# Four sums of weight quarters made by adding transfers that GpSimd begins, in a two-layer hybrid decoder on one Trainium2 core

## The chip, the core and the metric

The kernel runs on one core of a Trainium2 chip. A core has five engines that run their own in-order queues and meet at semaphores: TensorE (PE, with its weight loads shown as PEld), VectorE (DVE), ScalarE (ACT), GpSimd (POOL) and SyncE (SP). Sixteen DMA engines move data between HBM and the on-chip memory SBUF, or within SBUF. TensorE writes its sums to the small memory PSUM. The metric is the device time of one execution in microseconds; lower is better.

## The reference

Two layers, each one pre-norm mixer with three head groups that share one input projection. Cut to what matters here:

```python
def _layer(x, ...):
    h = _rmsnorm(x, norm_g)
    proj = h @ w_in            # (512, 2048) @ (2048, 7696)
    ...
    mix = jnp.concatenate([y_conv, y_sb, y_gla], axis=-1)
    return x + mix @ w_out     # (512, 2048) @ (2048, 2048)

for l in range(2):
    h = _layer(h, ...)
```

The change touches only how the weights of the last product, `mix @ w_out`, are prepared.

## The kernel before

Every projection is cut into tiles of 256 output columns. A tile of weights is 2048 x 256 in float32; it is fetched by two SyncE transfers of 1 MB into a staging buffer `st` of shape 128 x 16 x 272 (`fetch`, line 332; there are two such buffers). ScalarE squares it to find its size (`wmax`, line 347), GpSimd adds over the partitions (`wscale`, line 355, the all-reduce of line 362), VectorE turns that into a scale of a power of two (lines 363 to 379), and then each value is split into a float16 high part, made by ScalarE, and a float16 low part, made by VectorE. A product of two split numbers takes three float16 matmuls. The tiles of split weights, `wh` and `wl`, come in three buffers each. `weights()` (line 467) is called at each tile: it starts the fetch of the tile two ahead and the splitting of the next one. A staging buffer is free for its next fetch when the last split that reads it is done.

The output projection of a layer has eight column groups. In groups 3, 4 and 6 of the first layer and 3, 4, 5 and 6 of the second (`QUICK`, line 30), seven in all, the product is made from 2 x 2 blocks with seven block products in place of eight (`project_quick`, line 686; its matmuls are line 698, 48 for each product, 336 for a group). For this the weights enter as the four quarters b11, b12, b21, b22, each a 128 x 8 x 128 view of the staging buffer in rows of 512 bytes, and as sums of them. `wsums` (line 436) makes these sums in place and splits them: part 0 is b11, part 3 is b22, part 1 is b11 + b12 + b22, part 2 is b12 + b22, part 4 is b21, part 5 is b11 + b12, part 6 is b11 + b12 + b22 + b21. Parts 0 and 1 share one pair of weight buffers, 2 and 3 the next, 4 and 5 the third; part 6 has its own small pair (`e` and `ga`). A split is one ScalarE instruction (line 450) and one VectorE instruction (line 451). The sums depend on each other through the quarters that they overwrite. The products are written in the source in the order of parts 0, 1, 2, 3, 4, 5, 6; ScalarE and VectorE carry the partial results out of PSUM on the way (lines 709 to 727), and line 1247 adds the residual.

Outside the kernel's first stretch a scheduler puts the instructions of each engine in order when the program is built. It places them by times that it assumes, so a change of one instruction also moves others. In the program before, GpSimd begins no transfers; SyncE and ScalarE do.

Of the kernel before, what the change touches and what calls it, by code (L numbers as in the profile page):

```python
# [11 lines left out]
ALU = mybir.AluOpType  # L12
# [27 lines left out]
def hybrid_trunk(ctx, tc, x, norm_g, w_in, conv_w, conv_b, sb_qn_g, sb_kn_g,  # L40
                 gla_w_up, gla_b_up, gla_on_g, w_out, out):
    nc = tc.nc
    V, S, G, T = nc.vector, nc.scalar, nc.gpsimd, nc.tensor
# [23 lines left out]
    def nm(s):  # L67
        uid[0] += 1
        return f"{s}_{uid[0]}"
# [4 lines left out]
    def wk(shape, tag, bufs=None, dt=F32):  # L74
        return work.tile(shape, dt, tag=tag, name=nm(tag), bufs=bufs)
# [347 lines left out]
    def load_(i):  # L423

        with tc.issue_after(lasthi[i - 1].ins):
            for h in range(2):
                wmax(i, h)
        wscale(i)
        if i in quick:
            wsums(i)  # L430
            return
        for h in range(2):
            whi(i, h)
            wlo(i, h)

    def wsums(i):

        sc = scales[i]
        b11, b12, b21, b22 = (whole[i][:, r::2, c * P:(c + 1) * P] for r in range(2) for c in range(2))
        parts = loaded[i][0]  # L440
        for _ in range(3):
            a = [wpool.tile([P, HK, GX], F16, tag=t, name=nm(t)).rearrange("p k c -> p (k c)") for t in ("wh", "wl")]
            parts.extend([p_[:, n * HK * P:(n + 1) * HK * P] for p_ in a] for n in range(2))
        parts.append([wk([P, HK * P], t, dt=F16) for t in ("e", "ga")])
        for n in range(7):
            parts[n] = [a.rearrange("p (k c) -> p k c", c=P) for a in parts[n]]

        def split(b, n):
            h_, l_ = parts[n]
            hi = S.activation(h_, b, AF.Copy, scale=sc)  # L450
            V.scalar_tensor_tensor(l_, b, sc, h_, ALU.mult, ALU.subtract)  # L451
            return hi


        split(b11, 0)
        V.tensor_tensor(b11, b11, b12, ALU.add)
        split(b22, 3)
        V.tensor_tensor(b12, b12, b22, ALU.add)
        V.tensor_tensor(b22, b11, b22, ALU.add)
        split(b22, 1)  # L460
        lasthi[i] = split(b12, 2)
        V.tensor_tensor(b22, b22, b21, ALU.add)
        split(b21, 4)
        split(b11, 5)
        split(b22, 6)
# [845 lines left out]
```

## Time and profile before

| | before |
|---|---|
| median of 3 runs | 1720.0 us (1718.39 to 1720.52) |
| the profiled execution | 1721.89 us |
| its span | 1720.1 us |
| TensorE clock granted, mean | 0.997 |
| DMA, mean over the span | 205 MB, 119 GB/s |
| HBM read, written | 173.36 MB, 8.39 MB |

All rows of the trace come from one execution. Its span is the time between the first and the last instruction; 1.8 us lie around it. A row of a group of instructions gives line, engine, operation, output and input tile with buffer numbers left out, count, then busy time and the mean duration of one in ns, and the idle time of the engine ahead of them with what ended it. A row of the waits names who waited for whom, the total in us, how often, and the longest. A row of the windows gives the stretch, its length, the busy time of PE, PEld, VectorE, ScalarE and GpSimd with the number of instructions, the granted clock, the share of time in which the DMA engines were busy, and GB/s. A row of the timeline or of the chain of waits begins with start and length in us from the start of the span. A row of a transfer ends with the median time from its issue until the data has landed.

### The profile page before, as it was taken

To read this page: it belongs to the slowest core of one execution; us is meant where nothing else is said; L and a number is where in the kernel's file an instruction comes from. 1 tells how busy PE (TensorE), PEld (TensorE's weight loads), DVE (VectorE), ACT (ScalarE), POOL (GpSimd) and SP (SyncE) were. 2 spreads that over 40 slices of the span, in tenths; PEclk is the share of its full clock that TensorE was granted. 3 is DMA by queue.
4 is the path that set the end of the run, shared out by engine and by line. 5 is a ranking of instruction groups with operands and counts; after the bars stand their busy time and mean duration, and the time that the engine had idled before them with its cause. 6 is when DMAs were issued, how large, how long until landed. Compare 5 with 4: busy or idle time off the path is not lost. (4 is left out here: it accounts for less than half of the span.)

```text
span 1720.1 us, 32415 instructions
## 1 busy us (share of the span) xinstructions
PE 1702.0 (99%) x13770; PEld 1227.2 (71%) x13770; DVE 1166.7 (68%) x2149; ACT 1022.4 (59%) x1243; POOL 63.5 (4%) x104
## 2 busy tenths in 40 slices
PE   7999999999999999999999999999999999999998
PEld 5744557878787764799986454668686868548998
DVE  8566897566666656786675588974656566567883
ACT  7558676555555555566655575864555555545661
POOL 1100000000000000000010000000000000000000
PEclk9999999999999999999999999999999999999999
DMA  7323321344444445145544231223544433343441
GB/s 251 98 98 98 99 98 54 113 120 126 119 121 123 129 123 153 61 156 181 181 116 148 83 108 55 99 98 111 126 127 126 125 108 108 116 137 123 148 155 45
DMA packets 266641, 204.95 MB, mean 119 GB/s; under 512 B 93362, under 2 KB 265724, under 8 KB 265984
## 3 DMA queue, kind: packets, MB, share of 16 engines
q1 hardware_dynamic: 257488, 193.42, 37.1%
q10 hardware_dynamic: 9008, 9.45, 1.6%
q8 instruction: 108, 1.77, 0.4%
q14 instruction: 37, 0.30, 0.1%
HBM read 173.36 MB, written 8.39 MB: 106 GB/s over the span
## 5 line engine op out<-in xcount | busy, mean ns | idle before, releaser
L421 DVE SCALAR_TENSOR_TENSOR wl<-st,ws,wh 128x2048 f16<-128x2048 f32 (+1 forms) x138 | 324.4, 2352 | 205.3 <-ACT wh L415 205.3
L415 ACT ACTIVATE wh<-st,ws 128x2048 f16<-128x2048 f32 (+1 forms) x136 | 272.0, 2003 | 247.0 <-PE psp L633 111.0
L633 PE MATMUL psp<-wh,m 128*128 128x256 f16 x1216 | 331.5, 273 | 0.0
L632 PE MATMUL psp<-wl,m 128*128 128x256 f16 x1216 | 331.4, 273 | 0.0
L631 PE MATMUL psp<-wh,m 128*128 128x256 f16 x1216 | 331.4, 273 | 0.0
L352 ACT ACTIVATE junk<-st 128x2048 uint8<-128x2048 f32 (+1 forms) x150 | 285.5, 1903 | 4.9 <-DMA st<-in_w_out_dram 3.0
L633 PE MATMUL psp<-wh,x 128*128 128x256 f16 x768 | 209.3, 273 | 0.0
L632 PE MATMUL psp<-wl,x 128*128 128x256 f16 x768 | 209.3, 273 | 0.0
L631 PE MATMUL psp<-wh,x 128*128 128x256 f16 x768 | 209.3, 273 | 0.0
L623 PE MATMUL psp<-m,wh 128*128 128x512 f16 x512 | 194.0, 379 | 0.0
L624 PE MATMUL psp<-x,wh 128*128 128x512 f16 x512 | 194.0, 379 | 0.0
L624 PE MATMUL psp<-m,wh 128*128 128x512 f16 x512 | 194.0, 379 | 0.0
L623 PE MATMUL psp<-x,wh 128*128 128x512 f16 x512 | 194.0, 379 | 0.0
L625 PE MATMUL psp<-x,wl 128*128 128x512 f16 x512 | 193.9, 379 | 0.0
L625 PE MATMUL psp<-m,wl 128*128 128x512 f16 x512 | 193.9, 379 | 0.0
L625 PEld LDWEIGHTS <-wl 128*128 128x128 f16 x1024 | 100.2, 98 | 119.7
L624 PEld LDWEIGHTS <-wh 128*128 128x128 f16 x1024 | 100.2, 98 | 118.7 <-issue 2.6
L623 PEld LDWEIGHTS <-wh 128*128 128x128 f16 x1024 | 100.2, 98 | 117.5 <-issue 1.9
L631 PEld LDWEIGHTS <-m 128*128 128x128 f16 x1216 | 119.0, 98 | 13.9
L633 PEld LDWEIGHTS <-m 128*128 128x128 f16 x1216 | 119.0, 98 | 13.9
L632 PEld LDWEIGHTS <-m 128*128 128x128 f16 x1216 | 119.0, 98 | 13.8
L363 DVE TENSOR_SCALAR wq<-wgm 128x1 f32<-128x1 f32 x75 | 15.9, 212 | 111.1 <-POOL wgm L362 111.1
(356 smaller groups left out, 2665.0 us busy)
## 6 DMA issues: line engine op xcount, KB each, us to landing
st<-in_w_in_dram SPq DMA_DIRECT2D x120, 1024.0 KB, 7.7
st<-in_w_out_dram SPq DMA_DIRECT2D x32, 1024.0 KB, 7.6
x<-in_x_dram SPq DMA_DIRECT2D x4, 1024.0 KB, 5.1
qT<-in_x_dram ACTq DMA_DIRECT2D x8, 512.0 KB, 6.4
qT<-xs ACTq DMA_DIRECT2D x8, 512.0 KB, 3.9
xs<-x SPq DMA_DIRECT2D x14, 256.0 KB, 3.8
out_dram<-kT SPq DMA_DIRECT2D x14, 256.0 KB, 2.1
th<-za SPq DMA_TRANSPOSE x64, 3.1
```

The lines of the kernel that those rows point to most:

```text
L352: S.activation(junk(HK * n).rearrange("p (k n) -> p k n", k=HK), staged[i][h][:, :, :n], AF.Square, accum_out=peak[i][:, h:h + 1])
L363: V.tensor_scalar(m, gm[:, 0:1], gm[:, 1:2], 2.0 ** -120, ALU.add, ALU.max)
L415: lasthi[i] = S.activation(wh[:, :, :n], staged[i][h][:, :, :n], AF.Copy, scale=scales[i])
L421: V.scalar_tensor_tensor(wl[:, :, :n], staged[i][h][:, :, :n], scales[i], wh[:, :, :n], ALU.mult, ALU.subtract)
L623: T.matmul(o, wh[:, kk, cs], xh[:, :, k, :], start=st_, stop=False)
L624: T.matmul(o, wh[:, kk, cs], xl[:, :, k, :], start=False, stop=False)
L625: T.matmul(o, wl[:, kk, cs], xh[:, :, k, :], start=False, stop=en)
L631: T.matmul(o, ah[:, t, k, :], wh[:, kk, :n], start=st_, stop=False, skip_group_check=True)
L632: T.matmul(o, ah[:, t, k, :], wl[:, kk, :n], start=False, stop=False, skip_group_check=True)
L633: T.matmul(o, al[:, t, k, :], wh[:, kk, :n], start=False, stop=en, skip_group_check=True)
```

## The change

In `wsums` the four VectorE additions become four transfers that GpSimd begins. Each reads one quarter and adds it into another, in the same places of the staging buffer as before; the splits and their source order stay.

```diff
         split(b11, 0)
-        V.tensor_tensor(b11, b11, b12, ALU.add)
+        G.dma_start(out=b11, in_=b12, accum_op=ALU.add)
         split(b22, 3)
-        V.tensor_tensor(b12, b12, b22, ALU.add)
-        V.tensor_tensor(b22, b11, b22, ALU.add)
+        G.dma_start(out=b12, in_=b22, accum_op=ALU.add)
+        G.dma_start(out=b22, in_=b11, accum_op=ALU.add)
         split(b22, 1)
         lasthi[i] = split(b12, 2)
-        V.tensor_tensor(b22, b22, b21, ALU.add)
+        G.dma_start(out=b22, in_=b21, accum_op=ALU.add)
         split(b21, 4)
         split(b11, 5)
         split(b22, 6)
```

With the new times that the scheduler assumes, the built program also has other orders inside the seven groups. On TensorE the matmuls are the same, but the products of part 2 come ahead of those of part 1 and those of part 4 are partly ahead of part 3. On ScalarE and VectorE the splits of parts 4 and 5 come earlier among the splits of a group, and those of parts 2 and 1 later. On GpSimd the 28 transfers stand between the all-reduces of line 362; those of one group follow each other, and in five groups the all-reduce of the next tile stands between the third and the fourth, in two behind the fourth. Outside these groups the orders are the same but for a few neighbours.

## The prediction

> **What bounds the kernel now.** I read the busy shares of the page first, then the waits of the tensor engine, then the stretches in which seven-product groups run (windows of 20 us), then the chain of waits at the end.
>
> ```profile
> span 1720.1 us, 32415 instructions
> PE 1702.0 (99%) x13770; PEld 1227.2 (71%) x13770; DVE 1166.7 (68%) x2149; ACT 1022.4 (59%) x1243; POOL 63.5 (4%) x104
> ...
> PE psp L698 <- ACT g L709: 1.3, 1, 1.3
> PE psp L698 <- DVE g L711: 0.8, 1, 0.8
> PE psp L698 <- DVE wl L451: 0.2, 1, 0.2
> ```
>
> TensorE is busy in 99% of the span. In all seven groups (matmul line 698) it waits for the other engines 1.3 + 0.8 + 0.2 = 2.3 us. So whatever VectorE is relieved of, no more than 2.3 us can come back there: 1720.0 - 2.3 = 1717.7 us.
>
> ```profile
> 1640.00:1660.00 20.00, 20.00 (x362) 20.00 (x360) 17.04 (x25) 12.93 (x15) 0.40 (x1) 1.00 0.49 159
> 1660.00:1680.00 20.00, 19.84 (x354) 19.62 (x352) 16.88 (x24) 12.47 (x14) 0.40 (x1) 1.00 0.48 160
> ...
> 1664.71 9.15 DMA st<-in_w_out_dram
> 1673.95 2.00 ACT junk L352 x2
> 1675.95 1.05 ACT wh L450
> 1677.03 1.28 DVE wl L451
> ```
>
> The columns of the first two rows are the busy time of PE, weight load, VectorE, ScalarE and GpSimd, the clock and the DMA share. VectorE is busy 17 of 20 us and TensorE all 20: both are nearly full, with TensorE ahead. The chain rows show that a second loop closes almost as tightly: a staging buffer is released, 9.15 us of fetch, the maxima on ScalarE, the splits, release again. There is little room in which a longer splitting stage could hide.
>
> **What is removed.**
>
> ```profile
> L456 DVE TENSOR_TENSOR st<-st x7: 1218/1225/1226, 764.9 to 1665.8; 128x1024 f32<-128x1024 f32 x7
> L462 DVE TENSOR_TENSOR st<-st x7: 1216/1218/1224, 773.6 to 1679.8; 128x1024 f32<-128x1024 f32 x7
> L451 DVE SCALAR_TENSOR_TENSOR wl<-st,ws,wh x42: 1273/1278/1286, 762.5 to 1681.7; 128x1024 f16<-128x1024 f32 x42
> L450 ACT ACTIVATE wh<-st,ws 128x1024 f16<-128x1024 f32 x42 | 46.4, 1141 | 23.4 <-PE psp L698 9.7 <-DVE st L458 6.0 <-PE psp L633 3.0
> ```
>
> Four additions in each of seven groups, 28 x 1.22 = 34 us of VectorE. By the 2.3 us above, this is worth next to nothing on the path.
>
> **What is added: 28 transfers that form one chain.** Number them 1 to 4 in each group (lines 456, 458, 459, 462). Transfer 2 overwrites b12, which transfer 1 reads; transfer 3 adds b11 (result of 1) into b22, which transfer 2 reads; the split of part 1 reads the result of 3; transfer 4 overwrites b22 after that split. In the built program transfer 2 waits for the semaphore of 1, transfer 3 for that of 2, transfer 4 for that of 3 and for VectorE's half of split 1. So no two of a group overlap. With D the time from start to landing of one transfer, and a split costing 1.14 us on ScalarE plus 1.28 us on VectorE, that is 2.42:
>
> split 0 (2.42), three transfers (3D), split 1 (2.42), transfer 4 (D), ScalarE's half of split 6 (1.14) = 4D + 6.0 us from split 0 to the end of split 6.
>
> Does the next group have to wait for it? ScalarE is an in-order queue. In the order the built program gives it, split 6 of group 3 of the second layer stands ahead of split 0 of group 4, and that of group 4 ahead of split 0 of group 5: there the period is 4D + 6.0. Between groups 5 and 6 of that layer and between 3 and 4 of the first, split 0 comes ahead of split 6. In the first layer GpSimd's queue has transfer 4 ahead of the all-reduce that scales the next group, so split 0 follows the issue of transfer 4: 3D + 2.42 + 2.42 + 1.06 = 3D + 5.9, the 1.06 being the path from the all-reduce to split 0 (778.85 to 779.91 below). In the second, split 0 of group 6 needs the weight tile that parts 0 and 1 of group 5 share, so it follows product 1 of group 5, 16.09 / 6 = 2.7 us (six products in the row of 1619.05) after split 1: 3D + 2.42 + 2.42 + 2.7 = 3D + 7.5.
>
> ```profile
> 778.85 0.40 POOL L362 PARTITION_ALL_REDUCE wgm<-wm  x1 [18.26 <-ACT junk L352]
> 779.91 1.15 ACT L450 ACTIVATE wh<-st,ws 128x1024 f16<-128x1024 f32 x1 [0.88 <-DVE ws L375]
> ...
> 761.31 2.19 ACT L450 ACTIVATE wh<-st,ws 128x1024 f16<-128x1024 f32 x2 [1.21 <-DVE wp L377]
> 817.22 0.19 ACT L352 ACTIVATION_READ_ACCUMULATOR junk<-st 128x1 f32 x1
> 818.62 1.15 ACT L450 ACTIVATE wh<-st,ws 128x1024 f16<-128x1024 f32 x1 [1.21 <-DVE wp L377]
> 849.89 0.42 DVE L727 TENSOR_TENSOR g<-psp,g 128x256 f32<-128x256 f32 x1
> ...
> 1605.52 1.13 ACT L450 ACTIVATE wh<-st,ws 128x1024 f16<-128x1024 f32 x1
> 1619.05 16.09 PE psp L698 x288
> 1695.58 0.42 DVE L727 TENSOR_TENSOR g<-psp,g 128x256 f32<-128x256 f32 x1 [0.80 <-PE psp L698]
> ```
>
> *Second layer, groups 3, 4, 5, 6 in a row.* Split 0 of group 3 starts at 1605.52; nothing ahead of it changes. Before, the last product of group 6 ended at 1695.58 (the VectorE instruction that reads it). After: 1605.52 + two periods of 4D + 6.0, one of 3D + 7.5, then 4D + 6.0 for group 6, VectorE's half of split 6 (1.28) and the last product, 2.7: 1605.5 + 15D + 25.5 + 4.0 = 1635.0 + 15D. Delay 15D - 61.
>
> *First layer, groups 3 and 4, then 6.* Group 3's split 0 stays at 761.31, group 4's comes 3D + 5.9 later, its split 6 another 4D + 6.0: 773.2 + 7D. Group 6 loads into the buffer that group 4 gives back (two staging buffers): VectorE's half (1.28), a fetch, the second maximum (2.1, the 1.91 and 0.19 of line 352), and 1.2 from there to split 0 (817.4 to 818.62). The fetch takes 9.5 us in this stretch (rows below). Then 4D + 6.0 + 1.28 + 2.7. Sum 773.2 + 7D + 14.1 + 4D + 10.0 = 797.3 + 11D, before 849.89: delay 11D - 53.
>
> Together 26D - 114 us. The 114 us is the slack that covers the chain today; it is spent at D = 4.4 us, and each further microsecond of D costs 26.
>
> Queued behind the waiting instructions: on GpSimd the all-reduce of the next tile, which I have counted where it decides; on ScalarE and VectorE, behind splits that wait for a transfer, the evictions of the products of the running group (lines 709 to 727), so TensorE also waits for PSUM banks; but it would at that time be waiting for the weights anyway. SP's fetches stand behind the split that frees their buffer; with 9.5 + 2.1 + 1.2 = 12.8 us against the 3D that runs beside them, they stay covered for D over 4.3 us. The products are put in another order on TensorE, with the same 336 matmuls a group: nothing.
>
> **How long is D?** No transfer that adds, none between two places of SBUF without a transpose, and none begun by GpSimd is in the trace. The nearest rows (the two of the first layer's stretch, 735 to 900 us, come first):
>
> ```profile
> qT<-in_x_dram ACTq DMA_DIRECT2D x5, 512.0 KB, 8.0
> st<-in_w_out_dram SPq DMA_DIRECT2D x8, 1024.0 KB, 9.5
> ...
> qT<-xs ACTq DMA_DIRECT2D x8, 512.0 KB, 3.9
> L362 POOL PARTITION_ALL_REDUCE wgm<-wm x75 | 34.4, 458 | 1407.5 <-ACT junk L352 1316.7 <-DVE wl L421 72.2 <-DVE g L721 18.5
> ```
>
> Each addition reads 512 KB and the old 512 KB of the target and writes 512 KB. A plain 512 KB takes 3.9 us where little else moves, 8.0 in this very stretch beside the fetches. Lower end: 3.9, if reading the target costs nothing. Upper end: one pass at 8.0, two more at 3.9 if the second read and the addition hide nowhere, and an all-reduce's 0.46 to start on GpSimd: 16.3. I take 9.5, the row whose 1024 KB equal the two reads and which was measured in this stretch. 26 x 9.5 - 114 = 133 us. The profiled execution took 1721.9 us (1.8 around its span of 1720.1), the median of three is 1720.0; on the median: 1853 us.
>
> The Trainium skill, "DMA: Bandwidth & Descriptors", section "Anatomy of one DMA — SWDGE (gpsimd) path", gives for a plain transfer begun by GpSimd 2.0 us plus the bytes over 436 GB/s, an estimate of 3.2 us for 512 KB. By it 26D - 114 is below zero and the change would cost nothing. No run here shows a transfer begun by GpSimd; the 8.0 us row for the same bytes speaks against using it under this load.
>
> **The rivals.**
> 1. *Not slower.* The adding transfer lands as fast as a plain one on quiet queues, D = 3.9: 26 x 3.9 - 114 is -13, so the slack covers it all and the time stays at 1720, at best 1717.7. It decides below D = 4.4. For it: DMA is half idle (share 0.48). Against: 8.0 us for the same bytes, and a second read. 0.07.
> 2. *GpSimd or the adding path is the bound.* Each quarter is 128 x 8 rows of 512 bytes, 1024 pieces; if GpSimd's making of these, or the additions in the DMA engines, takes longer than moving, D is not set by bytes. It decides above the 16.3; at D = 20: 1720 + 406 = 2126 us. For it: GpSimd is the engine with the least measured work (64 us) and no row bounds such work. 0.11.
> 3. *Relief wins.* Transfers covered and VectorE's 34 us let the evictions run sooner: 1717.7. It needs rival 1 and the 2.3 us. 0.02.
>
> **How the numbers follow.** Forecast (chain of transfers, D from 5, a plain pass and 1 us, to 16.3): 0.77, with 1720 + 16 = 1736 to 1720 + 310 = 2030 us. Unnamed, between rival 1 and the forecast: 0.03. The range is the forecast's own, 1736 to 2030, and leaves out about 2 in 10, most of it rival 2. A measurement of this kernel tells 0.2% (3.4 us) from no change. Slower: 0.77 + 0.11 + the unnamed 0.03 = 0.91; of the 0.09 of rivals 1 and 3 I give 0.06 to no change and 0.03 to faster.
>
> **What would show it.** DMA issues at lines 456 to 462 with their landing time: D itself; 9.5 is the guess, 26 us per microsecond the test of the chain. In the waits, TensorE's line 698 should wait some 130 us for ScalarE's line 450 and VectorE's line 451, and these for DMA into the staging tile. VectorE's busy time should fall by 34 us to about 1132. The distance from split 0 of group 4 to that of group 5 in the second layer should be 4D + 6. It is wrong if two transfers of a group overlap, if the loss is in stretches without such groups, or if D is over 5 and the time has not moved.

## The result, and the profile after

| | before | after |
|---|---|---|
| median of 4 runs each, in turn | 1720.26 us | 1823.24 us |
| lowest to highest | 1718.39 to 1721.29 | 1820.64 to 1827.86 |
| ratio of the times, 95% interval | | 1.0603 (1.058 to 1.0626) |
| mean granted TensorE clock | 0.997 | 0.975 |

The change costs 103 us. The forecast was 1853 us, a loss of 133, with a range of 1736 to 2030 us. First the page of the kernel after: busy times, then the transfers that GpSimd begins (packets and MB of their queue, and the median landing time).

```profile
span 1821.5 us, 32485 instructions
...
PE 1718.7 (94%) x13770; PEld 1241.4 (68%) x13770; DVE 1135.9 (62%) x2121; ACT 1022.9 (56%) x1243; POOL 106.5 (6%) x132
...
q0 software_dynamic: 29120, 14.68, 7.0%
...
st<-st POOLq DMA_DIRECT2D x28, 512.0 KB, 6.5
```

VectorE is relieved of 1166.7 - 1135.9 = 30.8 us, and that buys nothing. TensorE executes the same 13770 matmuls, yet is busy 1718.7 - 1702.0 = 16.7 us longer. The rest is in its waits, of which this is the view after:

```profile
PE psp L698 <- ACT wh L450: 39.9, 6, 17.2
PE psp L698 <- ACT g L709: 35.3, 6, 10.8
PE psp L698 <- DVE wl L451: 5.2, 6, 1.1
...
PE psp L698 <- DVE g L711: 3.2, 1, 3.2
```

With two further rows of 1.8 and 0.8 us for evictions (lines 717 and 713), line 698 waits 86.2 us where it waited 2.3: 83.9 us more. With the 16.7 that is 100.6 of the 101.4 us by which the span grew. The windows after show where:

```profile
740.00:920.00 180.00, 142.57 (x1721) 132.16 (x1719) 87.00 (x131) 90.86 (x138) 24.23 (x21) 0.91 0.70 157
1600.00:1660.00 60.00, 60.00 (x555) 53.81 (x553) 43.51 (x46) 25.60 (x22) 6.61 (x4) 1.00 0.50 138
...
1720.00:1740.00 20.00, 5.05 (x91) 4.93 (x89) 7.20 (x10) 2.98 (x4) 3.09 (x2) 0.71 0.94 207
```

TensorE was full in the windows shown of before. Now the first layer's stretch has it busy 142.57 of 180 us, where it was 175.66 before, and one window of the second layer 5.05 of 20, at a granted clock of 0.71. Up to the first split that waits for a transfer, the second layer runs as before (60 of 60 us). The chain of waits after, in the second layer, groups 3 and 4 and the beginning of 5 (start, length, what):

```profile
1649.23 5.88 DMA st<-st
...
1655.46 6.17 DMA st<-st
...
1662.21 6.18 DMA st<-st
...
1671.39 6.61 DMA st<-st
...
1682.38 10.58 DMA st<-st
...
1693.31 6.16 DMA st<-st
...
1700.07 6.76 DMA st<-st
...
1709.68 7.32 DMA st<-st
...
1721.05 13.51 DMA st<-st
```

These are the four transfers of each group, end to end, as in the prediction's formula. In the four groups of this layer 14 of the 16 lie on the chain, together 105.7 us, 7.55 each. Of all 28 transfers, 19 take 5.9 to 6.8 us; 10.58 and 13.51 are first transfers, which run while a fetch of line 341 does (begun at 1680.52 and 1719.52). From group 4's first to group 5's first pass 38.7 us: 30.8 of transfers and 7.9 of splits and hand-offs.

The rows of the VectorE instruction that reads the last product of each layer's groups tell what each layer lost:

```profile
890.44 0.42 DVE L727 TENSOR_TENSOR g<-psp,g 128x256 f32<-128x256 f32 x1 [0.79 <-PE psp L698]
...
1797.72 0.42 DVE L727 TENSOR_TENSOR g<-psp,g 128x256 f32<-128x256 f32 x1
```

The first comes 40.6 us later than before (849.89), the second 102.1 us later (1695.58): the first layer lost 40.6 us and the second 61.6, where the forecast's two sums gave 11 x 9.5 - 53 = 51.5 and 15 x 9.5 - 61 = 81.5.

### The profile page after: what moved, and what is told of

Same layout as the page of the kernel before. It is cut to its first block, busy times and chain, and to the rows that moved or that the text cites. A ratio compares the mean times of both kernels' runs of the same rounds, so it can differ in the third digit from the quotient of the medians.

```text
span 1821.5 us, 32485 instructions
## 1 busy us (share of the span) xinstructions
PE 1718.7 (94%) x13770; PEld 1241.4 (68%) x13770; DVE 1135.9 (62%) x2121; ACT 1022.9 (56%) x1243; POOL 106.5 (6%) x132
## 3 DMA queue, kind: packets, MB, share of 16 engines
q0 software_dynamic: 29120, 14.68, 7.0%
## 4 chain that ended last, share of the span: by engine, by line
PE 40%; DMA 7%; DVE 1%; issue 1%; ACT 1%; SPq 0%; POOLq 0%; DVEq 0%
PE psp L624 6%; PE psp L623 6%; PE psp L625 6%; DMA st<-st 6%; PE psp L631 5%; PE psp L633 5%; PE psp L632 5%; PE psp L738 3%; PE psp L698 1%; PE psz L913 1%; PE psm L1153 1%; PE psz L1116 1%; DMA st<-in_w_out_dram 0%; DMA m<-raw 0%; DVE x L655 0%
## 5 line engine op out<-in xcount | busy, mean ns | idle before, releaser
L362 POOL PARTITION_ALL_REDUCE wgm<-wm x75 | 34.3, 457 | 1320.7 <-ACT junk L352 1224.9
```

Source lines behind the costliest of these rows:

```text
L362: G.partition_all_reduce(gm, peak.pop(i), P, RED.add)
```

## The experiments

All times are medians of four runs, the loss is against the kernel before on the same chip in the same rounds. "Wait" is TensorE's in the matmul line of the products (698; edits shift its number), "busy" TensorE's busy time (2.3 and 1702.0 before); the landing time is the median of the transfers that GpSimd begins. Half, eighth, plain, smallfetch and smallboth leave out a part of the sums or of the weights; they are read for time alone.

| kernel | landing, us | time, us | loss, us | ratio, 95% interval | wait | busy |
|---|---|---|---|---|---|---|
| changed | 6.5 | 1823.24 | 103.0 | 1.0603 (1.058 to 1.0626) | 86.2 | 1718.7 |
| half | 4.2 | 1778.21 | 57.5 | 1.034 (1.032 to 1.0359) | 41.8 | 1718.6 |
| eighth | 2.3 | 1742.80 | 23.8 | 1.0138 (1.0123 to 1.0153) | 17.5 | 1708.2 |
| plain | 4.0 | 1765.89 | 45.2 | 1.0268 (1.0253 to 1.0283) | 30.9 | 1717.0 |
| twohalves | 5.0 | 1804.28 | 83.7 | 1.0488 (1.0472 to 1.0504) | 65.1 | 1721.9 |
| only4 | 7.3 | 1734.86 | 15.9 | 1.0091 (1.0076 to 1.0106) | 17.4 | 1701.3 |
| first3 | 6.5 | 1804.69 | 84.1 | 1.0493 (1.0475 to 1.051) | 67.9 | 1719.9 |
| smallfetch | 6.4 | 1803.10 | 82.5 | 1.0481 (1.0466 to 1.0497) | 62.5 | 1721.1 |
| smallboth | 2.3 | 1729.79 | 9.2 | 1.0058 (1.0043 to 1.0073) | 8.2 | 1704.3 |
| side | 6.8 | 1780.28 | 59.6 | 1.0349 (1.0333 to 1.0365) | 38.2 | 1711.6 |
| side4 | 12.4 | 1744.98 | 26.0 | 1.0149 (1.0132 to 1.0165) | 17.8 | 1706.6 |
| freegp | 6.5 | 1832.86 | 113.9 | 1.0662 (1.0646 to 1.0678) | 75.6 | 1726.8 |
| gadd | none | 1790.22 | 69.6 | 1.0411 (1.0395 to 1.0426) | 49.9 | 1717.6 |

### Smaller and plainer transfers

*half* and *eighth* cut each of the four transfers of a group in the same way (`:4`, and `:1` for eighth), *plain* drops the addition:

```diff
-        G.dma_start(out=b11, in_=b12, accum_op=ALU.add)
+        G.dma_start(out=b11[:, :4], in_=b12[:, :4], accum_op=ALU.add)
```

```diff
-        G.dma_start(out=b11, in_=b12, accum_op=ALU.add)
+        G.dma_start(out=b11, in_=b12)
```

> The four transfers add only the first four of the eight blocks of rows (half of each sum is left out): 256 KB and 512 rows each, the same number of transfers and waits. Theory A with a landing time that goes with bytes: 4.0 to 4.6 us where no fetch runs, 5 with those beside fetches, 26 x 5 - 114 = 16, so 1720 to 1745 us. If the landing time is mostly a fixed cost of beginning and ending, it stays above 5.5 and the time above 1765 us.

> The four transfers of a group copy in place of adding (the sums are left out), with the same places, waits and queue. If the adding sets the landing time of 6 to 7 us, a plain one lands in 4 to 5 us, the slack of 4.4 us covers nearly all of it, and the time is 1718 to 1745 us. If GpSimd's making of 1024 rows of 512 bytes sets it, the landing time stays at 6 us or more and the time at 1800 us or more.

> The four transfers add only the first of the eight blocks of rows (64 KB each; seven eighths of each sum are left out): number, waits and queue as in the changed kernel, the landing time small, 2 to 3 us. Theory A (landing times in a chain, 26D - 114, spent at 4.4 us): covered, 1718 to 1728 us. Theory D (what costs is mostly the built order and the hand-offs between the queues, since the halved transfers with landing times near 4.2 us cost 57 us where A gave 16): 1740 us or more, TensorE still waiting 20 us or more in line 698.

The landing times came out as expected (4.2 us for half, 2.3 for eighth). But the times did not: half lost 57.5 us where its expectation had 26 x 5 - 114 = 16, and eighth 23.8 us where the formula gives less than nothing. Between eighth and the changed kernel the loss grows by (103.0 - 23.8) / (6.5 - 2.3) = 18.9 us per microsecond, and half lies near that line, 57.5 against 59.7 (23.8 + 1.9 x 18.9). Carried down, the line meets zero at 2.3 - 23.8 / 18.9 = 1.04 us. These are medians; with the means of the 28 transfers (3.1, 5.0 and 7.3 us) the slope is the same, and zero lies at 1.8 us. No run has a landing time between VectorE's 1.22 us and 2.3, so where the loss begins is an estimate. Eighth shows that a slack up to 4.4 us was not there. Its chain of waits in the second layer shows what binds beside the transfers:

```profile
1649.05 6.04 PE psp L698 x76
1655.17 1.16 ACT wh L450
1656.35 1.30 DVE wl L451
...
1657.94 6.38 DMA st<-st
...
1664.60 2.87 DMA st<-st
...
1668.55 1.80 ACT junk L352
...
1670.53 1.05 ACT wh L450
...
1673.19 3.80 DMA st<-st
```

Here the chain runs through TensorE itself: a split starts as a run of TensorE's products ends, and only then the group's first transfer (6.38 us, since a fetch runs beside it); the maxima of a later tile stand in ScalarE's queue ahead of the next splits. So preparation waits for TensorE here. That a lead can therefore not be kept from one group for the next is read from this chain; no run tests it alone.

Plain's landing time of 4.0 us tells what the addition adds. The rows of plain's queue and of its transfers:

```profile
q0 software_dynamic: 4032, 14.68, 2.6%
...
st<-st POOLq DMA_DIRECT2D x28, 512.0 KB, 4.0
```

The same 14.68 MB went in 4032 packets in place of 29120: with the addition nearly every packet is one row of 512 bytes (1024 of the 1040 of a transfer), and the transfer lands 2.5 us later. Whether the number of packets takes this time, or the reading and adding of the target, no run separates. A copy alone is still no way out, at 45.2 us. That is 10.7 us under what the line above gives for 4.0 us (23.8 + 1.7 x 18.9 = 55.9), so the landing time is not all that counts; the rest stays open.

### Cut in two

```diff
+        def add2(o, i_):
+            for ks in (slice(0, 4), slice(4, 8)):
+                G.dma_start(out=o[:, ks], in_=i_[:, ks], accum_op=ALU.add)
...
-        G.dma_start(out=b11, in_=b12, accum_op=ALU.add)
+        add2(b11, b12)
```

The other three likewise.

> The changed kernel with each transfer cut in two of 256 KB, one after the other in GpSimd's queue (56 transfers), the second half of one sum beside the first half of the next where the waits allow it. If a transfer's time is mostly a fixed part (a landing time of 4.2 us for half, 6.2 for the whole), the halves overlap and the time falls to 1770 to 1805 us. If the pieces of 512 bytes set it, or the waits of GpSimd's queue keep the halves one behind the other: 1815 us or more.

1804.28 us, at the edge of the first case: the overlap exists and is worth 19 us (103.0 - 83.7), with 5.0 us for a half where one alone took 4.2. The number of rows and of bytes stays, and most of the loss too.

### Which of the four

*only4* leaves sum 4 a transfer and gives the first three back to VectorE; *first3* is the opposite, with this edit:

```diff
-        G.dma_start(out=b22, in_=b21, accum_op=ALU.add)
+        V.tensor_tensor(b22, b22, b21, ALU.add)
```

> Only the fourth sum of each group is a transfer (7 transfers, none waits for another; the first three sums on VectorE). Theory A: a group's chain is 3 x 1.22 + 6.5 + 6 = 16.2 us, under the 23.6 us at which the slack is spent: 1718 to 1728 us. If a single transfer at the end of a group's chain already costs, as a split behind evictions in VectorE's queue would show, 1735 us or more.

> Transfers 1 to 3 as in the changed kernel, the fourth sum on VectorE (1.22 us). Theory A with 7.5 us for a transfer: second layer 12 x 7.5 + 3.7 - 61 = 33, first layer 9 x 7.5 + 2.4 - 53 = 17, with TensorE's lower clock some 8 more: 1765 to 1785 us. If the end of a group (sum 4, the last split, the buffer's release) is what counts: under 1755 us.

Both lost more than the formula gave, again: 15.9 us where none, and 84.1 where 33 + 17 + 8 = 58 were expected. Together they make 100.0 of the 103.0 us, so the parts add. Only4's chain of waits in the second layer shows a loop that a single transfer stretches:

```profile
1618.98 6.96 DMA st<-st
1625.96 1.16 ACT e L450
...
1628.89 8.87 DMA st<-in_w_out_dram
1637.84 2.00 ACT junk L352 x2
1639.85 1.05 ACT wh L450
...
1642.50 7.26 DMA st<-st
...
1665.10 7.36 DMA st<-st
```

Transfer 4 delays the last split, which frees the staging buffer; the fetch into it follows, the maxima of what it brings stand in ScalarE's queue ahead of the next group's splits, and on one of those the next transfer 4 waits: 23.5 us around, and 22.6 the next time. Before, the last splits of groups 3 to 5 began 23.8 us apart (the first at 1617.38) and then 19.9:

```profile
1641.17 1.15 ACT L450 ACTIVATE e<-st,ws 128x1024 f16<-128x1024 f32 x1 [0.25 <-DVE st L462]
...
1661.04 1.15 ACT L450 ACTIVATE e<-st,ws 128x1024 f16<-128x1024 f32 x1 [1.36 <-DVE st L462]
```

So the first turn is no longer than before and the second is 2.7 us longer, of the 6 us by which such a transfer exceeds the addition: most of it is covered, but not all, though the formula saw slack for the whole. This is the second loop that the prediction's first part saw as closing "almost as tightly", and then counted only ahead of the first layer's group 6.

### The fetches

*smallfetch* shortens the weight fetches of the seven groups, *smallboth* does so on top of eighth:

```diff
-        whole[i] = stage.tile([P, KT, GX], F32, tag="st", name=nm("st"))
-        for h in range(2):
+        few = i in quick or {i - 1, i + 1} <= quick
+        whole[i] = whole[i - 2] if few else stage.tile([P, KT, GX], F32, tag="st", name=nm("st"))
+        for h, ke in ((0, 1 if few else HK), (1, 1 if few else HK)):
...
-                    s_[:, :, o:o + w],
-                    src[l, h * HK * P:(h + 1) * HK * P, c0:c0 + w].rearrange("(k p) n -> p k n", p=P))
+                    s_[:, :ke, o:o + w],
+                    src[l, h * HK * P:(h * HK + ke) * P, c0:c0 + w].rearrange("(k p) n -> p k n", p=P))
```

> The changed kernel, but the fetches of the seven groups' tiles (and of the one tile between them) bring one of eight blocks of rows into the same two staging buffers (seven eighths of these weights are left out). Theory F (much of the loss comes from the fetches: a group's late end frees its staging buffer late, the fetch then runs beside the next group's first two transfers, which land in 10 to 14 us instead of 6.2, and the maxima of the fetched tile stand in ScalarE's queue ahead of splits): all transfers land in 6 to 6.6 us, 26 x 6.3 - 114 = 50, and 1765 to 1785 us. If the fetches beside them don't matter: 1810 us or more.

> The kernel eighth (transfers of 64 KB) with the short fetches of the kernel smallfetch. Theory F: the 24 us that eighth still cost were its first transfers beside fetches (5.4 against 2.3 us) and the late fetches themselves: 1718 to 1727 us. Theory D (the built order and the hand-offs alone): 1735 us or more.

Both kernels lie between their two cases, with 1803.1 us and 1729.79. The long first transfers went (the medians of the four are 6.2 to 6.6 us; one second transfer still took 11.8), and the fetches account for 103.0 - 82.5 = 20.5 us of the loss, 23.8 - 9.2 = 14.6 us of eighth's. But 62.5 us of wait remain in smallfetch where the formula gave 50, most of it in one row:

```profile
PE psp L698 <- ACT g L709: 40.8, 7, 11.3
```

With short fetches and short transfers together 9.2 us are left, and that is the most which the built order, the hand-offs and GpSimd's starts of the transfers can be charged with in that kernel.

### Transfers that no split waits for, and GpSimd's queue

*side* leaves the sums to VectorE and begins as many transfers aside, all into one target in HBM, so that each waits in GpSimd's queue for the one before; *side4* has four targets (`offs[n]`) and no such wait. Both first write their targets once. Cut:

```diff
+    off = dram.tile([P, HK, P], F32, tag="off", name="off")
+    def aside(a):
+        G.dma_start(out=off, in_=a, accum_op=ALU.add)
...
+        a = sm(P, "aside", bufs=2)
+        V.tensor_scalar(a, ident, sc, None, ALU.mult)
+        a = a.rearrange("p (o c) -> p o c", o=1).to_broadcast([P, HK, P])
...
-        G.dma_start(out=b11, in_=b12, accum_op=ALU.add)
+        V.tensor_tensor(b11, b11, b12, ALU.add)
+        aside(a)
```

> VectorE makes the four sums as in the kernel before, and beside them GpSimd begins the same 28 adding transfers of 512 KB, each waiting for the one before it, into a target in HBM that no split reads (28 transfers are added, none is waited for by the splits). Theory A (the loss is the chain: the splits wait for one transfer after the other): 1718 to 1728 us, TensorE idle in line 698 under 6 us, granted clock 0.99 or more. Theory B (the loss is the load on the DMA engines, or the fetches that these transfers hold up): 1760 us or more, with the stretches of the seven groups longer by 15 us or more each and waits of line 698 that go back to fetches. Theory C (the all-reduces that stand behind the transfers in GpSimd's queue): 1740 us or more, with the maxima's all-reduce of line 362 as the releaser of the splits.

> VectorE makes the sums, and GpSimd begins the 28 transfers of 512 KB aside, as in the kernel side, but into four targets, so that no transfer waits for another in GpSimd's queue. Theory C (side's 60 us come from the all-reduces that stand behind transfers which wait for each other): without these waits 1718 to 1732 us. Theory B (contention for the DMA engines, which stays or grows as four transfers run at once): 1760 us or more.

Side was a miss for theory A: 59.6 us lost, though no split waits for a transfer. The timeline of its GpSimd (the last columns are the idle time before an instruction and what ended it):

```profile
760.53 0.40 POOL L362 PARTITION_ALL_REDUCE wgm<-wm  x1 [23.36 <-ACT junk L352]
762.19 1.52 POOL L411 DMA_DIRECT2D off<-aside  x1 [1.26 <-DVE wu L379]
768.55 1.45 POOL L411 DMA_DIRECT2D off<-aside  x1 [4.84 <-DMA off<-aside]
...
782.77 1.44 POOL L411 DMA_DIRECT2D off<-aside  x1 [6.39 <-DMA off<-aside]
783.58 1.00 POOL L362 PARTITION_ALL_REDUCE wgm<-wm  x1
```

The next tile's all-reduce stands behind all four and comes at 783.58; before, it came at 778.85. Without the waits, side4 loses 26.0 us, so the waits in the queue make some 34 us of difference. Side4 falls between its two cases. Of the 26.0, the four first writes explain about 4 (TensorE is busy 726.74 us of the first 740, and 730.81 before). For the rest, side4's chain of waits in the second layer names the fetches:

```profile
1628.50 20.83 DMA st<-in_w_out_dram
...
1659.87 14.38 DMA st<-in_w_out_dram
...
1684.99 12.71 DMA st<-in_w_out_dram
```

Beside four such transfers a fetch takes 12.7 to 20.8 us, not the 9.15 of before: the transfers and the fetches slow each other when transfers run four at once (side4's own land in 12.4 us). In the changed kernel no two of a group run at once, and of two groups only one pair does, for 1.6 us. Whether GpSimd's queue counts there too is what *freegp* asks: TensorE makes the sums over partitions for the groups' tiles and the tile behind each.

```diff
-        if i:
+        if i - 1 in quick or i in quick:
+            ps = bank(psm, "m")[:, :1]
+            pk = peak.pop(i)
+            for j in range(2):
+                T.matmul(ps, ones.to_broadcast([P, P]), pk[:, j:j + 1], start=j == 0, stop=j == 1)
+            V.tensor_scalar(m, ps, 2.0 ** -120, None, ALU.max)
+        elif i:
```

> The changed kernel, but the sums over partitions for the seven groups' tiles and the tile behind each are made by TensorE (two one-column matmuls and a VectorE read) and not by GpSimd, so that no scale stands behind a transfer in GpSimd's queue. Theory A (the transfers of a group and the splits between them are the chain): 1812 to 1828 us, since split 0 of a group still follows split 6 of the group before it. Theory C (the queue of GpSimd is the chain, as in the kernel side): 1795 us or less.

No gain: 1832.86 us, above both cases. In its waits the products (here line 704) wait 75.6 us, 10.6 less than in the changed kernel, and TensorE now waits for the maxima itself:

```profile
PE psp L704 <- ACT wh L456: 56.9, 6, 16.2
PE psm L364 <- ACT junk L352: 11.7, 2, 7.8
```

The edit alters TensorE's queue too, so it settles only this: taking the all-reduces out of GpSimd's queue does not bring the time back, and most of the wait stays with the splits of line 450 (456 here), which wait for transfers. The trace of the changed kernel itself tells where the queue counts. Of the seven all-reduces that stand behind a group's third or fourth transfer, one begins with no idle time behind the start of a transfer, in the first layer; the other six wait for ScalarE's maxima. The rows of that one and of one of the six:

```profile
787.29 1.00 POOL L362 PARTITION_ALL_REDUCE wgm<-wm  x1
...
1666.89 0.40 POOL L362 PARTITION_ALL_REDUCE wgm<-wm  x1 [3.13 <-ACT junk L352]
```

So GpSimd's queue holds a scale back at one place, the one that the prediction counted. What it costs there no run shows alone.

### The sums as GpSimd additions

```diff
-        G.dma_start(out=b11, in_=b12, accum_op=ALU.add)
+        G.tensor_tensor(b11, b11, b12, ALU.add)
```

> The four sums are GpSimd additions (28 instructions of 128 x 1024 f32), no transfers. Theory A with the duration of such an addition in the place of D: under 4.4 us each it is covered and the time is 1718 to 1728 us; at 6 us each it is 26 x 6 - 114 = 42 us more. Rival: GpSimd's additions slow VectorE's splits (1.28 us before) by more than 0.1 us each, and the time goes over 1728 us though the additions take under 4.4 us.

An addition takes 2.4 us, and yet 69.6 us are lost. GpSimd's timeline shows a cost that neither theory had:

```profile
766.41 0.40 POOL L362 PARTITION_ALL_REDUCE wgm<-wm  x1 [23.63 <-DMA xs<-x]
773.52 2.34 POOL L456 TENSOR_TENSOR st<-st 128x1024 f32<-128x1024 f32 x1 [6.72 <-issue]
775.94 2.35 POOL L458 TENSOR_TENSOR st<-st 128x1024 f32<-128x1024 f32 x1
...
794.36 0.41 POOL L362 PARTITION_ALL_REDUCE wgm<-wm  x1 [5.86 <-issue]
```

At each change from an all-reduce to an addition or back GpSimd stands idle, here for 6.72 and 5.86 us, "issue", with nothing that it waits for. The Trainium skill, "GPSIMD Engine Reference", section "Instruction dispatch", puts some 6 us on the first call of newly loaded code; these gaps agree in length, but the trace does not show that code is loaded in them. The rival of the expectation holds in part: the splits of line 451 into `wl` took 1438 ns on average, 1282 in the changed kernel, but the median stayed at 1280; seven of the 42, which began beside an addition of GpSimd's, took 1565 to 2942 ns. The run says nothing on transfers, but shows GpSimd's own arithmetic to be no substitute beside these all-reduces.

## Why the prediction came out as it did

- **Direction and mechanism: right.** The transfers of a group follow one another, the splits wait for them, TensorE's line 698 waits for lines 450 and 451 and for evictions (line 709) that stand behind such splits. The evictions have 41.1 of the 86.2 us of wait, but of the second layer's chain only 0.42 us (line 711 at 1680.41), as the prediction said. The loss lies in the two stretches of the seven groups: TensorE is busy 730.78 us of the first 740, and 730.81 before. VectorE's relief is worth nothing.
- **D = 9.5 us: too large.** It was taken from the row of a 1024 KB fetch. It is 5.9 to 6.8 us for 19 of the 28, 7.3 on average, 7.55 on the second layer's chain. The second read did not come at the price of a second 512 KB. Half and eighth show a time that grows with the rows and bytes, 1.9 us from 128 rows to 512 and 2.3 to the whole 1024.
- **The slack of 114 us, spent at D = 4.4: too large,** and this is the step that failed. The sum let split 0 of the first group stay, strung everything behind it on one chain, and set what this chain had in hand over several groups against what the transfers add. Eighth lost 23.8 us at a median of 2.3 where this gives less than nothing; half, plain and only4 lost more than it gives too. What the chains of eighth and only4 have in its place are loops from one group to the next, through TensorE's products, the fetches and the maxima. That these are also why the slope was 18.9 and not 26 is argued, not shown.
- **These errors cancel, so the nearness of 133 to 103 is in part luck.** With the median that was measured, the formula would have given 26 x 6.5 - 114 = 55, with the 7.55 of the chain 82; the loss was 103. Layer by layer, with the means of their own transfers (7.1 us over the first layer's twelve, 7.55 on the second's chain), the two sums give 25 and 52 us, where 40.6 and 61.6 were lost. By the line that the runs gave, carried on beyond them, 9.5 us would have cost some (9.5 - 1.04) x 18.9 = 160 us, by the means some 145, not 133. That 82 is close to the 83.9 us of added wait holds only there, where transfers fill most of the chain.
- **Covered fetches: right for the chain, but not harmless.** In the second layer no fetch stands on the chain between group 3's first transfer and group 6's last. But a fetch slows the transfer beside it (10.58, 13.51), which the sum left out; shortening the fetches gave back 20.5 us.
- **Not foreseen: TensorE's lower clock,** 16.7 us of busy time.
- **Smaller ones.** In the second layer 14 transfers lie on the chain and not 15: two fourth ones are covered, where the sum had one, and 13.50 us of products run at the end instead of 2.7. The period from group 4 to 5 is 30.8 us of transfers and 7.9 of the rest, where 6.0 were counted: 0.35 us pass from one landing to the next issue, 0.55 ahead of a third transfer. VectorE's busy time fell by 30.8 us and not by 34.
- **The rivals.** "Not slower" fell with its price as well as its threshold: the landing time is not 3.9 us, and at 2.3 the kernel is still slower. GpSimd's share in beginning a transfer is 1.55 us of 6.5, and the adding makes it 2.5 us longer than plain; both are far under the 16.3 us from which that rival decides. "Relief wins" had nothing to win.

None of these versions beats the kernel before. The nearest one that computes everything, only4, is 0.91% behind it (0.76 to 1.06).

## What to carry to other kernels

Ask of a slack whether it can be saved up: where buffers tie preparation to the consumer group by group, a lead that is added up over several groups says more than is there. Here up to 4.4 us for a transfer were thought free, and transfers of 2.3 us already cost 23.8 us. Price the small version too: had the formula been held against a transfer of 2 us, its "nothing" would have had to be defended. And moving work from a busy engine to an idle one pays only where the busy engine is what others wait for; here it turned 1.22 us into 6.5 in the middle of a ring.

## What the runs showed of the hardware

**TensorE's clock falls when it waits long.** Of the matmuls of line 698 that take the high part and the operand `raw`, grouped by form, first before:

```profile
L698 PE MATMUL psp<-wh,raw 128*128 128x128 f16 x112 | 19.2, 219 | 1.3 <-ACT g L709 1.3
```

and after:

```profile
L698 PE MATMUL psp<-wh,raw 128*128 128x128 f16 x112 | 31.1, 287 | 52.5 <-ACT g L709 35.3 <-ACT wh L450 17.2
```

The same 112 matmuls have 52.5 us of idle time ahead of them and take 287 ns in place of 219; the window after of 1720 to 1740 us, shown above, has the clock at 0.71. The Trainium skill, "TensorE: Matmul & The Clock Gate", section "What's actually happening", has the clock halved after an idle window of about 3.4 us. These waits of up to 17.2 us agree, and the trace's clock record holds only 1.0 and 0.5. So a long wait of TensorE costs more than its length: 83.9 us of wait brought 16.7 us of slower matmuls. Only4's wait of 17.4 us brought none (1701.3 us busy); its longest single wait in the products was 3.8 us. Eighth's 17.5 us, with one wait of 4.2, brought 6.2 (1708.2).

**An adding transfer is not a plain one.** For 512 KB between two places of SBUF in rows of 512 bytes it took 1040 packets (29120 / 28) where the plain one took 144, 6.5 us against 4.0, and 1.55 us of GpSimd's time against 0.88. Beside a fetch it took up to 13.5 us. The estimate of 3.2 us for a plain one, from the Trainium skill, "DMA: Bandwidth & Descriptors", section "Anatomy of one DMA — SWDGE (gpsimd) path", is 0.8 us under what plain measured.
